# Attention on one core: where GpSimd splits the queries, and where it adds up the modulation

## The chip, the cores and the metric

One Trainium2 chip, one core. The metric is the time on the device in microseconds (us) of one execution. An execution takes 2790.1 us (median of 3, 2789.61 to 2793.39).

## What is computed

An encoder trunk of two layers on a sequence of 1024 positions, width 1024, in float32. The first layer mixes positions by grouped-query attention, the second by a gated unit; each is followed by a squared-ReLU MLP, and each sub-layer is normalised and modulated (shift, scale, gate) by a conditioning vector. What matters here, cut from the reference:

```python
cond = jax.nn.silu(c)
for i in range(DEPTH):                                   # 2
    mod = cond @ ada_w[i] + ada_b[i]                     # 6 x 1024 values
    sh1, sc1, g1, sh2, sc2, g2 = jnp.split(mod, N_MOD, axis=-1)
    ...
def one_block(q_blk):                                    # 16 heads of 64, 4 key heads
    s = jnp.einsum('bqkgd,bskd->bkgqs', q_blk, k).astype(jnp.float32) * scale
    p = jax.nn.softmax(s, axis=-1).astype(v.dtype)
    return jnp.einsum('bkgqs,bskd->bqkgd', p, v)
```

## The kernel before

TensorE multiplies operands of a reduced kind of float32, so every operand is split in two parts, a rounded one ("hi") and the rest ("lo"), and products of the parts are added in PSUM. Splitting is work for ScalarE, VectorE and GpSimd.

The attention loop (line 920) runs over 64 units. Unit i is one head and 256 queries; four units in a row (i mod 4 = 0 to 3) share one key head and one group of 256 queries. The stages of a unit are spread over three iterations, and the order of all instructions is written out by hand, in a string of twenty steps that each iteration goes through (line 1588):

```python
ORDER = "s00 v20 t10 q10 h10 t11 e00 s01 h11 t12 h12 v21 t13 e01 h13 v22 v23 q00 f20 m00"
```

The letter is the stage; the first digit says whose it is (0: unit i, 1: unit i-1, 2: unit i-2). Most instructions are pinned to this order; the split of the queries is not pinned, but instructions on one engine run one behind the other.

- s (line 834): scores, four matmuls of 512 columns; VectorE takes their maximum (line 837).
- e (line 843): the exponential, on ScalarE. t (line 851): its transposes on TensorE, copied by ScalarE to the rounded part (line 854). h (line 860): the rest, on VectorE.
- v (line 870): product with the values; ScalarE copies the two halves (lines 880 and 882), and f (line 887) joins them on GpSimd.
- q with w = 0, near the end of an iteration: `q_stage` on GpSimd, for the next group of four units. Per half of the 256 queries it makes the rounded part (line 811) and the rest (line 812), so four instructions per call, into two tiles of the pool "t" (58 tiles of 128x512).
- q with w = 1, near the start of the iterations with i mod 4 = 2 and 3: `q_trans`, four pinned transposes on TensorE (line 820) of what `q_stage` made, and a copy by ScalarE (line 823). The result is used from the next i mod 4 = 0 on.
- m, the last step of an iteration: first, in the opening units, some deferred work (rotary positions of the last queries: lines 567 and 569 on VectorE, 570 and 583 on GpSimd); in units 53 to 62 preparation for the output product; then `slabs.step`.

`slabs.step` works off 32 steps of the modulation of the second layer, four groups of eight. Where its second argument is true it takes one step:

```python
self.ahead(3)                                            # loads, 512 KB each, SP's queue
...
if dt == 0:
    pin(G.tensor_scalar(self.acc[g], raw, condc[:, 0:1], None, ALU.mult))            # line 182
else:
    pin(G.tensor_scalar(raw, raw, condc[:, dt : dt + 1], None, ALU.mult))            # line 184
    pin(G.tensor_tensor(self.acc[g], self.acc[g], raw, ALU.add))                     # line 185
```

`ahead(3)` keeps up to three loaded tiles (the present step's and two more), of four buffers. Three iterations after the eighth step of a group, eight small matmuls close it (line 194).

The q step with w = 0 stands ahead of f and m in an iteration. So on GpSimd a unit's order is: split (if any), join, deferred work, modulation step (if any).

Of the kernel before, what the change touches and what calls it, by code (L numbers as in the profile page):

```python
# [36 lines left out]
def encoder_kernel(ctx: ExitStack, tc: tile.TileContext, t: dict, out: bass.AP):  # L37
# [16 lines left out]
    def slot(dt=F32, shape=(P, 512)):  # L54
        return mem.tile(list(shape), dt, tag="t", name=nm("t"), bufs=SLOTS["t"])
# [24 lines left out]
    def f32(ap):  # L80
        return ap.bitcast(F32)
# [119 lines left out]
    slabs = Slabs([(1, 1), (1, 0), (1, 2), (1, 4)])  # L201

    def mods(n, tag="w"):
        for _ in range(min(n, len(pending))):
            layer, j, k = pending.pop(0)
            mod_load(layer, j, k, tag)
            if j in (1, 4):
                mod_scale(layer, j // 3, k)
# [252 lines left out]
    def load_x(hf, k):  # L461
        x_ = xslot()
        nc.sync.dma_start(x_, t["xT"][k * P : (k + 1) * P, hf * HALF : (hf + 1) * HALF])
        return x_
# [292 lines left out]
    def load_sel():  # L757
        for i in range(2):
            raw, s_ = slot(F32, (32, 512)), slot(F32R, (32, 512))
            nc.sync.dma_start(raw, t["sel"][:, i * 512 : (i + 1) * 512])  # L760
            V.tensor_copy(s_, raw)
            sel.append(s_)

    def wo_sums(hf):
        ri = small.tile([P, 4, NH], F32, tag="ri", name=nm("ri"), bufs=1)
        V.reciprocal(ri, rowsum[:, 4 * hf : 4 * hf + 4])
        rs = small.tile([P, 4, 2, NH], F32R, tag="rs", name=nm("rs"), bufs=1)
        V.tensor_copy(rs[:, :, 0], ri)
        V.tensor_tensor(rs[:, :, 1], ri, f32(rs[:, :, 0]), ALU.subtract)
        pt = bank_x("rt", (32, 512), F32R)  # L770
        for j in range(4):
            T.transpose(pt[:, j * P : (j + 1) * P], rs[:, j].rearrange("p s h -> p (s h)"), identr)
        rT[hf] = slot(F32R, (32, 512))
        S.copy(rT[hf], f32(pt))

    def wo_prep(hf, dt):
        pb = bank_x("bc")
        T.matmul(pb, sel[dt // 4][:, (dt % 4) * P : (dt % 4 + 1) * P], rT[hf], start=True, stop=True)
        o_ = ot.pop((dt, hf))
        V.tensor_tensor(o_, o_, pb, ALU.mult)  # L780
        hi, lo = slot(F32R), slot(F32R)
        S.copy(hi, o_)
        (G, V)[hf].tensor_tensor(lo, o_, f32(hi), ALU.subtract)
        on[(dt, hf)] = (hi, lo)

    def wo_mm(m, halves, bank):
        wh, wl = load_w("wo", m)
        ps = {hf: bank("wo") for hf in halves}
        for hf in halves:
            for k in range(KT):  # L790
                hi, lo = on[(k, hf)]
                T.matmul(ps[hf], wh[:, k], hi, start=k == 0, stop=False)
                T.matmul(ps[hf], wh[:, k], lo, start=False, stop=False)
                T.matmul(ps[hf], wl[:, k], hi, start=False, stop=k == KT - 1)
        for hf in halves:
            V.scalar_tensor_tensor(x[hf][m], ps[hf], mod[:, 0, 2, m : m + 1], x[hf][m], ALU.mult, ALU.add)
            (sqA, sqB)[hf].add(x[hf][m])
# [4 lines left out]
    with ExitStack() as es:  # L802

        def q_stage(qq, g):
            qh = []
            for j in range(2):
                q_ = qn[(2 * qq + j, g // 2)]
                src = q_[:, (g % 2) * 256 : (g % 2) * 256 + 256].rearrange("p (h d) -> p h d", h=4)
                d_ = slot(F32R)
                dv = d_.rearrange("p (h s d) -> p h s d", h=4, s=2)  # L810
                G.tensor_copy(dv[:, :, 0], src)
                G.tensor_tensor(dv[:, :, 1], src, f32(dv[:, :, 0]), ALU.subtract)
                qh.append(d_)
            return qh

        def q_trans(qh, hp, qst, bank=bank_x):
            pt = bank("qt", dt=F32R)
            for h in range(2):
                for j in range(2):
                    pin(T.transpose(pt[:, (2 * h + j) * P : (2 * h + j + 1) * P],  # L820
                                    qh[j][:, (2 * hp + h) * P : (2 * hp + h + 1) * P], identr))
            d_ = slot(F32R)
            pin(S.copy(d_, f32(pt)))
            qst.append(d_)
# [65 lines left out]
        units = []  # L890
# [7 lines left out]
        nu = len(units)  # L898

        qh = q_stage(0, 0)  # L900
# [19 lines left out]
        for i in range(nu + 2):  # L920
            u0 = units[i] if i < nu else None
            u1 = units[i - 1] if 0 < i <= nu else None
            u2 = units[i - 2] if i > 1 else None
            if u0:
                if i % 4 == 0:
                    qst, nxt = nxt, []
                u0.qst = qst
            for op in ORDER.split():
                f, w, j = op[0], int(op[1]), int(op[2])
                if f == "m":  # L930
                    if deferred:
                        deferred.pop(0)()
                    elif WO_AT <= i < WO_AT + 10:
                        if i == WO_AT:
                            load_sel()
                        elif i == WO_AT + 1:
                            wo_sums(0)
                        else:
                            wo_prep(0, i - WO_AT - 2)
                    elif i >= nu:  # L940
                        mods(1)
                    slabs.step(bank_x, i * 5 % 8 < 5)
                elif f == "q":
                    if i % 4 == 1 and w == 0 and i + 3 < nu:
                        qh = q_stage(units[i + 3].qq, units[i + 3].g)
                    if i % 4 > 1 and w == 1 and i + 2 < nu:
                        q_trans(qh, i % 4 - 2, nxt)
                else:
                    u = (u0, u1, u2)[w]
                    if u and (i or f not in "se"):  # L950
                        stages[f](u, j)
            if i == nu - 1:
                x[0] = [load_x(0, k) for k in range(KT)]
            if i == nu:
                wo_mm(0, (0,), bank_x)
# [308 lines left out]
    for ct in range(24):  # L1264
        i, r = divmod(ct, 3)
# [392 lines left out]
```

## Time and profile before

| | |
|---|---|
| median of 3 runs | 2790.1 us |
| profiled execution, its time | 2792.5 us |
| its span | 2790.5 us |
| mean granted clock of TensorE | 0.979 |
| TensorE busy, of the span | 2661.6 us, 95% |
| VectorE busy | 2269.1 us, 81% |
| ScalarE busy | 1459.8 us, 52% |
| GpSimd (POOL) busy | 1061.5 us, 38% |

"Busy" is the time in which an engine had an instruction in work. The granted clock is the share of TensorE's full clock that the chip allowed; at 0.5 a matmul takes twice as long. In the views of waits a row names who waited, at which line, and which engine and line ended the wait. In the timeline a row is one instruction or several alike (xN), with the idle time ahead of it in square brackets. PEld is TensorE's loading of the stationary operand, which runs beside the matmuls. The attention loop begins near 194 us and its last scores are made near 623 us.

### The profile page before, as it was taken

The numbers are of one execution on the slowest core, as the hardware profiler recorded it, in microseconds if no ns is written. First come the engines' busy times: TensorE is split into PE (matmuls) and PEld (weight loads), VectorE is DVE, ScalarE is ACT, GpSimd is POOL, SyncE is SP. The second block draws the span as 40 slices with busy tenths as digits, with TensorE's granted clock in tenths as the row PEclk, the third lists the DMA queues.
The fourth block names the chain that finished last, engine by engine and source line by source line (L and its number), as shares of the span: only waits on it lengthen the run. The fifth ranks groups of instructions, "written<-read, shape, count | busy, mean of one in ns | idle before, by whom it ended". The sixth has DMA issues, their size and how long they took to land. (4 is left out here: it accounts for less than half of the span.)

```text
span 2790.5 us, 37339 instructions
## 1 busy us (share of the span) xinstructions
PE 2661.6 (95%) x12804; PEld 2195.3 (79%) x12804; DVE 2269.1 (81%) x3191; ACT 1459.8 (52%) x2598; POOL 1061.5 (38%) x716
## 2 busy tenths in 40 slices
PE   7888999999899999999999999999999999999999
PEld 5667888888678887877778888887878688878877
DVE  7887777788888778998797777777998887788994
ACT  4447877893555555444453354444436554454442
POOL 2447656633520005452343355555551400034530
PEclk9899999999999999999999999999999999999999
DMA  7241111125245457744433245558732264478452
GB/s 260 68 144 39 50 50 54 33 91 178 79 157 193 146 187 288 276 171 149 147 121 108 95 157 178 178 182 298 285 117 87 85 206 162 145 255 290 151 194 75
DMA packets 200544, 427.52 MB, mean 153 GB/s; under 512 B 23137, under 2 KB 35425, under 8 KB 200354
## 3 DMA queue, kind: packets, MB, share of 16 engines
q1 hardware_dynamic: 173474, 387.37, 40.6%
q10 hardware_dynamic: 26880, 37.76, 3.7%
q8 instruction: 101, 1.65, 0.3%
q14 instruction: 89, 0.73, 0.1%
HBM read 306.56 MB, written 118.49 MB: 152 GB/s over the span
## 5 line engine op out<-in xcount | busy, mean ns | idle before, releaser
L1074 PE MATMUL out<-t,s 128*128 128x512 f32 x1232 | 486.8, 396 | 14.5 <-DVE t L288 14.5
L1073 PE MATMUL out<-t,s 128*128 128x512 f32 x1232 | 487.8, 396 | 8.8 <-ACT t L287 8.8
L1075 PE MATMUL out<-t,s 128*128 128x512 f32 x1232 | 485.9, 395 | 6.1 <-DVE s L1058 5.9
L415 PE MATMUL w<-t,s 128*128 128x512 f32 x1168 | 460.2, 395 | 0.5 <-ACT t L287 0.5
L416 PE MATMUL w<-t,s 128*128 128x512 f32 x1168 | 455.5, 391 | 1.4 <-DVE t L288 1.3
L417 PE MATMUL w<-t,s 128*128 128x512 f32 x1168 | 455.1, 390 | 1.0 <-DVE s L401 0.9
L288 DVE TENSOR_TENSOR t<-t,t 128x512 fp32r<-128x512 f32 x408 | 376.8, 937 | 29.4 <-ACT t L287 21.9
L287 ACT CAST t<-t 128x512 fp32r<-128x512 f32 x408 | 244.6, 618 | 154.5 <-DMA t<-hf 63.3
L400 ACT CAST s<-w 128x512 fp32r<-128x512 f32 x292 | 174.3, 619 | 227.4 <-PE w L417 155.5
L1074 PEld LDWEIGHTS out<-t,s 128*128 128x128 f32 x1232 | 234.8, 191 | 70.9 <-DVE t L288 21.8
L1073 PEld LDWEIGHTS out<-t,s 128*128 128x128 f32 x1232 | 234.7, 191 | 62.9 <-ACT t L287 13.9
L1075 PEld LDWEIGHTS out<-t,s 128*128 128x128 f32 x1232 | 234.7, 191 | 59.8 <-DVE s L1058 11.1
L401 DVE TENSOR_TENSOR s<-w,s 128x512 fp32r<-128x512 f32 x292 | 228.5, 791 | 62.9 <-ACT s L400 59.1
L1044 POOL TENSOR_TENSOR w<-w,t 128x512 f32<-128x512 f32 x32 | 51.6, 1615 | 558.9 <-DMA t<-hf 490.4
L416 PEld LDWEIGHTS w<-t,s 128*128 128x128 f32 x1168 | 219.4, 188 | 51.1 <-DVE t L288 6.5
L415 PEld LDWEIGHTS w<-t,s 128*128 128x128 f32 x1168 | 219.3, 188 | 50.1 <-issue 3.3
L1058 DVE TENSOR_TENSOR s<-t,s 128x512 fp32r<-128x512 f32 x240 | 216.0, 901 | 51.8 <-ACT s L1057 51.5
L417 PEld LDWEIGHTS w<-t,s 128*128 128x128 f32 x1168 | 219.2, 188 | 46.9 <-DVE s L401 2.1
L1057 ACT CAST s<-t 128x512 fp32r<-128x512 f32 x240 | 147.9, 621 | 190.9 <-PE out L1075 115.4
L837 DVE TENSOR_REDUCE mx<-s 128x1 f32<-128x1024 f32 x128 | 156.7, 1224 | 70.7 <-PE s L834 69.6
L860 DVE TENSOR_TENSOR t<-t,t 128x512 fp32r<-128x512 f32 x256 | 164.9, 684 | 22.2 <-ACT t L854 21.8
L854 ACT CAST t<-t 128x512 fp32r<-128x512 f32 x256 | 145.3, 592 | 39.5 <-PE t L851 37.1
(247 smaller groups left out, 5473.7 us busy)
## 6 DMA issues: line engine op xcount, KB each, us to landing
t<-hf SPq DMA_DIRECT2D x320, 256.0 KB, 4.5
hf<-c SPq DMA_DIRECT2D x156, 256.0 KB, 2.1
w<-in_wi_dram SPq DMA_DIRECT2D x64, 512.0 KB, 4.1
hf<-c ACTq DMA_DIRECT2D x96, 256.0 KB, 2.0
c<-in_ada_dram SPq DMA_DIRECT2D x36, 512.0 KB, 4.6
w<-in_adan_dram SPq DMA_DIRECT2D x32, 512.0 KB, 3.3
t<-in_wm_dram SPq DMA_DIRECT2D x64, 256.0 KB, 5.2
wf<-w SPq DMA_DIRECT2D x64, 256.0 KB, 3.2
```

The lines of the kernel that those rows point to most:

```text
L287: S.copy(hi, src)
L288: (eng or V).tensor_tensor(lo, src, f32(hi), ALU.subtract)
L400: S.copy(hi, src)
L401: V.tensor_tensor(lo, src, f32(hi), ALU.subtract)
L415: T.matmul(ps, hi[:, a], th, start=kt == 0, stop=False)
L416: T.matmul(ps, hi[:, a], tl, start=False, stop=False)
L417: T.matmul(ps, lo[:, a], th, start=False, stop=kt == 3)
L860: pin(V.tensor_tensor(lo, pt, f32(hi), ALU.subtract))
L1058: V.tensor_tensor(lo, src, f32(hi), ALU.subtract)
L1073: T.matmul(ps, hi[:, a], th, start=begin and kt == 0, stop=False)
L1074: T.matmul(ps, hi[:, a], tl, start=False, stop=False)
L1075: T.matmul(ps, lo[:, a], th, start=False, stop=end and kt == 3)
```

## The change

```diff
                     elif i >= nu:
                         mods(1)
-                    slabs.step(bank_x, i * 5 % 8 < 5)
+                    slabs.step(bank_x, i % 4 in (1, 2) or i % 8 == 3)
                 elif f == "q":
-                    if i % 4 == 1 and w == 0 and i + 3 < nu:
-                        qh = q_stage(units[i + 3].qq, units[i + 3].g)
+                    if i % 4 == 0 and w == 0 and i + 4 < nu:
+                        qh = q_stage(units[i + 4].qq, units[i + 4].g)
                     if i % 4 > 1 and w == 1 and i + 2 < nu:
                         q_trans(qh, i % 4 - 2, nxt)
```

`q_stage` for the next group of four is called in the first unit of a group instead of the second; 15 calls in both. The modulation steps were taken in the units with i mod 8 = 0, 2, 4, 5 and 7; they are now taken in those with i mod 8 = 1, 2, 3, 5 and 6. Both are five in eight units, until the 32 steps are done. `q_trans` stays where it was.

## Prediction, made before the changed kernel was run

> **What bounds the kernel now.** I read the page first, then the waits, then the attention stage unit by unit in the timeline, and last the busy table of single units. Rows of the page: engine, busy us, share, instructions.
>
> ```profile
> span 2790.5 us, 37339 instructions
> PE 2661.6 (95%) x12804; PEld 2195.3 (79%) x12804; DVE 2269.1 (81%) x3191; ACT 1459.8 (52%) x2598; POOL 1061.5 (38%) x716
> ```
>
> TensorE bounds the kernel as a whole, and GpSimd is busy for 38% only. An average over stages says nothing of a wait inside one stage, so the view of waits comes next (waiter, released by: us in total, times, longest).
>
> ```profile
> PEld qt L820 <- POOL t L812: 35.1, 25, 5.7
> PE qt L820 <- POOL t L812: 30.2, 24, 5.4
> ```
>
> L820 are the transposes of the split queries, pinned in TensorE's order; L812 is the last step of the split on GpSimd. So TensorE, the bound, stands still for 30.2 us because GpSimd, a mostly idle engine, is late. The timeline shows why. One stretch of GpSimd, then of TensorE, around unit 38 of the attention loop (time, busy us, engine, line):
>
> ```profile
> 450.85 0.72 POOL L887 TENSOR_TENSOR t<-t,t 64x256 f32<-64x256 f32 x1 [4.48 <-ACT t L882]
> 451.56 2.85 POOL L184 TENSOR_SCALAR w<-w,condc 128x1024 f32<-128x1024 f32 x1
> 454.49 2.39 POOL L185 TENSOR_TENSOR s<-s,w 128x1024 f32<-128x1024 f32 x1
> 456.83 0.74 POOL L811 CAST t<-t 128x256 fp32r<-128x256 f32 x2
> 457.54 1.40 POOL L812 TENSOR_TENSOR t<-t,t 128x256 fp32r<-128x256 f32 x2
> ```
>
> ```profile
> 458.31 0.28 PE L820 MATMUL qt<-identr,t 128*128 128x128 f32 x1 [1.74 <-POOL t L812]
> 459.00 0.45 PE L820 MATMUL qt<-identr,t 128*128 128x128 f32 x3 [0.40 <-POOL t L812]
> ...
> 459.92 2.06 PE L834 MATMUL s<-x,t 128*128 128x512 f32 x4
> ...
> 464.59 1.09 PE L834 MATMUL s<-x,t 128*128 128x512 f32 x4
> ```
>
> GpSimd first does the join of unit 36 (L887, 0.72 us), then a modulation step of unit 36 (L184 and L185, 451.56 to 456.88: 5.3 us), and only then the split of unit 37 (456.83 to 458.94: 2.1 us), whose transposes are due right at the start of unit 38. TensorE waits, and afterwards four score matmuls take 2.06 us where they take 1.09 us a little later. The busy table shows the same unit between a unit without and one with transposes (stretch, length, busy PE, PEld, DVE, ACT, POOL, then granted clock):
>
> ```profile
> 444.70:450.20 5.50, 5.50 (x42) 5.10 (x41) 4.93 (x7) 5.10 (x11) 1.59 (x2) 1.00 0.28 95
> 455.70:465.70 10.00, 7.86 (x46) 6.82 (x45) 5.03 (x6) 5.87 (x12) 9.22 (x8) 0.83 0.16 52
> 465.70:471.50 5.80, 5.80 (x46) 5.41 (x46) 4.94 (x6) 5.44 (x12) 0.73 (x1) 1.00 0.27 93
> ```
>
> A unit costs 5.5 us, with transposes 5.8, and there TensorE is busy throughout. The delayed one costs 10.0, and its clock was granted at 0.83 only.
>
> **The price of the delays.** I take the first score maximum of a unit (L837) as its start. Here are units 7, 35 to 40, 41 and 53:
>
> ```profile
> 247.49 1.23 DVE L837 TENSOR_REDUCE mx<-s 128x1 f32<-128x1024 f32 x1 [0.47 <-PE s L834]
> ...
> 438.87 1.23 DVE L837 TENSOR_REDUCE mx<-s 128x1 f32<-128x1024 f32 x1 [0.27 <-PE s L834]
> 444.69 1.23 DVE L837 TENSOR_REDUCE mx<-s 128x1 f32<-128x1024 f32 x1 [0.22 <-PE s L834]
> 450.19 1.23 DVE L837 TENSOR_REDUCE mx<-s 128x1 f32<-128x1024 f32 x1 [0.21 <-PE s L834]
> 455.70 1.23 DVE L837 TENSOR_REDUCE mx<-s 128x1 f32<-128x1024 f32 x1 [0.22 <-PE s L834]
> 465.72 1.23 DVE L837 TENSOR_REDUCE mx<-s 128x1 f32<-128x1024 f32 x1 [0.58 <-PE s L834]
> 471.54 1.22 DVE L837 TENSOR_REDUCE mx<-s 128x1 f32<-128x1024 f32 x1 [0.22 <-PE s L834]
> 478.83 1.23 DVE L837 TENSOR_REDUCE mx<-s 128x1 f32<-128x1024 f32 x1 [0.87 <-PE s L834]
> 555.03 1.23 DVE L837 TENSOR_REDUCE mx<-s 128x1 f32<-128x1024 f32 x1 [0.21 <-PE s L834]
> ```
>
> Units 36 and 37 take 5.50 and 5.51 us. Units 35 and 39 (i mod 4 is 3, second half of the transposes, never delayed) take 5.82. Unit 40, which closes a group of modulation sums with eight small matmuls, takes 7.29, that is 1.78 more than 5.51. Unit 38 takes 10.02, which is 4.20 too much: 2.1 us are waits (1.74 and 0.40), the other 2.1 us are slow matmuls behind them. From unit 7 to 53 there are 46 units, 23 of them with transposes, and three close a group. Without delays they would take 23 x 5.82 + 23 x 5.505 + 3 x 1.78 = 265.8 us. They took 555.03 - 247.49 = 307.5. So **41.7 us** of this stretch are delay, in the eleven units with i mod 4 = 2 from 10 to 50. This is more than the waits alone, because the slowed clock is in it.
>
> **The change part by part.** The split moves from the end of units 1, 5, 9... to the end of units 0, 4, 8...: the same 15 calls of four GpSimd instructions each, no DMA, nothing added. The modulation steps move from units 0, 2, 4, 5, 7 (mod 8) to 1, 2, 3, 5, 6: still five in eight, 32 in all, each with two GpSimd instructions (the first of a group one) and a 512 KB load on SP's queue.
>
> What GpSimd must do, by the durations above: step 5.3, join 0.73, split 2.1. In eight units that is 5 x 5.3 + 8 x 0.73 + 2 x 2.1 = 36.5 us, against 4 x 5.5 + 4 x 5.82 = 45.3 us that eight undelayed units take. It fits; the order decides.
>
> The split of i mod 8 = 4 is the tight one, as three steps in a row come before it. Count from the start of the unit after i mod 8 = 1. The join is released at +0.66 (450.19 to 450.85), so join and step end at 6.7; the second pair at 12.7; the third at 18.7 (6.03 each, longer than a unit, so a backlog builds). The split then ends at 20.8. The units passed are 5.82 + 5.82 + 5.5 + 5.5 = 22.6 us, and the transposes are due some 0.6 us into the next one, at about 23.2. It is ready **2.4 us early**. The split of i mod 8 = 0 has two steps and then an empty unit ahead of it: it ends at 15.5 on the same count, 7.7 us early. So all eleven delays go: -41.7 us. What is late next is nothing on GpSimd. Units then cost 5.82, as units 35 and 39 show, with TensorE busy throughout.
>
> The twelfth delay, the first in the stage, is different. At its start GpSimd also turns the last queries (L570, L583), and there the line-up is:
>
> ```profile
> 228.12 2.22 POOL L583 TENSOR_TENSOR t<-t,r 128x512 f32<-128x512 f32 x1
> ...
> 233.38 2.85 POOL L184 TENSOR_SCALAR w<-w,condc 128x1024 f32<-128x1024 f32 x1
> ...
> 238.59 0.75 POOL L811 CAST t<-t 128x256 fp32r<-128x256 f32 x2
> ...
> 240.08 0.37 PE L820 MATMUL qt<-identr,t 128*128 128x128 f32 x1 [5.41 <-POOL t L812]
> ```
>
> TensorE was ready at 234.7. Behind L583 (ends 230.34) the new order has the step of unit 3 (5.3, to 235.7), then the split. The first transpose started 1.5 us after the split's start (238.59 to 240.08), so it starts at 237.2: a wait of 2.5 us where there were 5.4. I take **-3 us**, with bounds 0 (the clock slows as before) and -6.8 (the whole delay of units 5 and 6 goes).
>
> The other edits cost nothing. The loads land in time:
>
> ```profile
> DMA to landing us min/median/max: 3.1/3.3/4.7
> ```
>
> Three steps in a row use one tile each 6.0 us, and each is requested two steps ahead; if that cover were gone a step would wait 3.3 us, beyond the 2.4 us in hand. The joins run up to 6 us later, but only the output product much later reads them. The four closings move by at most one unit and cost 1.78 us each as before.
>
> The slowed clock is where a rule can be weighed. The row of unit 38 shows 0.83 behind an idle time of 1.74 us. The Trainium skill (TensorE: Matmul & The Clock Gate, Part 1) says that the clock falls back after at least one idle window of about 3.4 us. By that rule gaps of 1.7 us would leave the clock alone, and the change would be worth the waits only; the row disagrees and I go by it.
>
> **Sum.** -41.7 - 3 = -44.7 us. The profiled execution took 2792.5 us (span 2790.5), so it would become 2747.8; against the median of 2790.1 that is **2745.4 us**. For the rest of the kernel I allow 4 us either way, as instructions that aren't pinned may shift; the forecast's own range is 2739 to 2753.
>
> **Rivals.**
> First, only the waits go and the slow clock stays, because it belongs to this stage and not to the waits. For: the matmuls of unit 38 stay slow well past the wait, beyond 459.92, so the slowness isn't the wait itself. Against: clock 1.00 in the undisturbed units above. It would give 30.2 less the 2.8 us still waited at the first split: 27.4, so 2762.7 us. The Trainium skill's window rule just cited points this way. Chance 0.08.
>
> Second, the three steps in a row eat the 2.4 us: the splits of i mod 8 = 4 stay late while those of 0 come free. That needs each step to take 0.8 us longer. Against:
>
> ```profile
> L583 POOL TENSOR_TENSOR t<-t,r x20: 1040/1047/2218, 81.6 to 232.4; 128x512 f32<-128x512 f32 x20
> L184 POOL TENSOR_SCALAR w<-w,condc x28: 2839/2846/2854, 220.5 to 545.1; 128x1024 f32<-128x1024 f32 x28
> ```
>
> The shortest and longest L184 (ns, minimum, median, maximum) are 0.5% apart wherever it ran. For: L583 took up to twice its median, once in the opening units (the 2.22 us above), so GpSimd work can slow. If late as now, five delays like unit 38's stay (at most 5 x 4.2 = 21 us): 2766 us. Chance 0.10. The Trainium skill (SBUF — State Buffer, Who interferes with whom) has GpSimd blocked by VectorE instructions with two SBUF inputs; L860 and L837, which read PSUM, wouldn't do it, so by that page this stage is safe.
>
> Third, on the slow side: the pool of 58 "t" tiles runs out. Each split holds two of them for one unit more; if none is free, the copy of the transposed weights (L854) waits a unit, 5.5 us, at each of 15 splits: +83, so 2790.1 - 44.7 + 83 = 2828 us. It decides from 3.0 us per split upwards (44.7 / 15). Against it is what L854 waits for now:
>
> ```profile
>   PE t L851: 37.1, 77
>   POOL s L185: 0.6, 2
> ```
>
> That is its own input, and hardly a freed tile. Chance 0.04.
>
> Fourth, the splits, which aren't pinned, are put behind the steps again, and nothing changes: 2790 us. Against: in all rows above they stand in the order of the program. Chance 0.03.
>
> **How the numbers follow.** Forecast 0.75, rivals 0.08, 0.10, 0.04, 0.03. The range takes the forecast's own range and reaches up to the first rival: 2738 to 2763, which leaves out the second rival, the last two and a little of the forecast. A measurement of this kernel tells about 0.2% (5.6 us) from no change. Forecast and first two rivals are faster by more: 0.93. Same 0.03, slower 0.04.
>
> **What would show it.** Right: the waits of qt L820 on POOL L812 fall from 30.2 to under 4 us, one near 235 us the longest; first score maxima of units 7 to 53 lie some 266 us apart; units of i mod 4 = 2 take 5.8 us at clock 1.00; GpSimd's busy time stays near 1061 us. Wrong: waits of 1 us or more at units 14, 22, 30, 38, 46 (second rival); clock below 1 between the waits (first); L854 waiting for a tile (third); L811 starting right behind L185 at units of i mod 4 = 2 (fourth).

## The result, and the profile after

The changed kernel takes **2743.78 us** (median of 4, 2740.23 to 2745.62), against 2789.86 before: ratio 0.9831, 95% interval 0.9814 to 0.9848. The forecast was 2745.4. The profiled execution took 2744.76 us, the page's first rows are:

```profile
span 2742.9 us, 37309 instructions
PE 2642.3 (96%) x12804; PEld 2184.9 (80%) x12804; DVE 2275.4 (83%) x3191; ACT 1454.5 (53%) x2598; POOL 1063.8 (39%) x716
```

GpSimd does the same work in the same time (1063.8 us against 1061.5); only its order is new. The view of the transposes' line (L820), its part on what they waited for:

```profile
its engine sat idle before it (us, times) until:
who waited for it (us, times):
```

Nothing stands under "sat idle": the 30.2 us of waits on the split are gone entirely. The starts of units 7, 38, 39 and 53 by their first score maximum, as shown for the kernel before:

```profile
243.81 1.23 DVE L837 TENSOR_REDUCE mx<-s 128x1 f32<-128x1024 f32 x1 [0.22 <-PE s L834]
...
422.79 1.23 DVE L837 TENSOR_REDUCE mx<-s 128x1 f32<-128x1024 f32 x1 [0.22 <-PE s L834]
428.61 1.23 DVE L837 TENSOR_REDUCE mx<-s 128x1 f32<-128x1024 f32 x1 [0.22 <-PE s L834]
...
509.68 1.23 DVE L837 TENSOR_REDUCE mx<-s 128x1 f32<-128x1024 f32 x1 [0.21 <-PE s L834]
```

Unit 38 now takes 428.61 - 422.79 = 5.82 us (10.02 before), what undelayed units with transposes took before. From unit 7 to 53 it is 265.87 us. The busy table of that stretch (length, PE, PEld, DVE, ACT, POOL, granted clock) has TensorE busy throughout and at full clock:

```profile
243.80:509.70 265.90, 265.90 (x1982) 247.70 (x1982) 229.45 (x284) 243.06 (x484) 200.02 (x149) 1.00 0.17 55
```

GpSimd around the tight split, that of unit 44 (44 mod 8 = 4), with the end of the third step ahead of it:

```profile
463.94 2.39 POOL L185 TENSOR_TENSOR s<-s,w 128x1024 f32<-128x1024 f32 x1
466.26 0.74 POOL L811 CAST t<-t 128x256 fp32r<-128x256 f32 x2
466.97 1.44 POOL L812 TENSOR_TENSOR t<-t,t 128x256 fp32r<-128x256 f32 x2
...
470.51 0.54 PE L820 MATMUL qt<-identr,t 128*128 128x128 f32 x4
```

The split ends at 468.41; its transposes start at 470.51 in unit 46, 2.1 us later. Where the time went, span against span: up to unit 7 the kernel is 247.49 - 243.81 = 3.7 us ahead, from unit 7 to 53 41.7 us, and in all that follows 2.3 us, which is within the spread of single runs. Together 47.6 us, of 2790.5 - 2742.9.

One thing is worse. In the opening, unit 3 takes 8.15 us (218.33 to 226.48). VectorE and GpSimd there:

```profile
218.33 1.21 DVE L837 TENSOR_REDUCE mx<-s 128x1 f32<-128x1024 f32 x1
...
223.59 2.97 DVE L569 TENSOR_TENSOR t<-t,t 128x256 f32<-128x256 f32 x2
223.88 2.39 POOL L185 TENSOR_TENSOR s<-s,w 128x1024 f32<-128x1024 f32 x1
...
226.48 1.21 DVE L837 TENSOR_REDUCE mx<-s 128x1 f32<-128x1024 f32 x1
```

The same place in the kernel before, where unit 3 took 5.93 us:

```profile
222.75 0.76 DVE L569 TENSOR_TENSOR t<-t,t 128x256 f32<-128x256 f32 x2
223.42 1.22 DVE L837 TENSOR_REDUCE mx<-s 128x1 f32<-128x1024 f32 x1
223.45 2.39 POOL L185 TENSOR_TENSOR s<-s,w 128x1024 f32<-128x1024 f32 x1
```

The two multiplies of L569 took 2.97 us instead of 0.76. Before, both were all but through (222.75 + 0.76 = 223.51) when L185 started on GpSimd at 223.45; after, L185 started between them, and the second ended only when L185 did. The score maximum queued behind it on VectorE came late, and ScalarE and TensorE behind it. The experiments had to settle two things: which half of the change does the work, and whether this reading of unit 3 holds.

### The profile page after: what moved, and what is told of

It is laid out like the page before. It is cut to its first block, busy times and chain, and to the rows that moved or that the text cites. A ratio compares the mean times of both kernels' runs of the same rounds, so it can differ in the third digit from the quotient of the medians.

```text
span 2742.9 us, 37309 instructions
## 1 busy us (share of the span) xinstructions
PE 2642.3 (96%) x12804; PEld 2184.9 (80%) x12804; DVE 2275.4 (83%) x3191; ACT 1454.5 (53%) x2598; POOL 1063.8 (39%) x716
## 5 line engine op out<-in xcount | busy, mean ns | idle before, releaser
L287 ACT CAST t<-t 128x512 fp32r<-128x512 f32 x408 | 244.3, 617 | 157.9 <-DMA t<-hf 65.2
L860 DVE TENSOR_TENSOR t<-t,t 128x512 fp32r<-128x512 f32 x256 | 164.3, 683 | 20.9 <-ACT t L854 20.9
L837 DVE TENSOR_REDUCE mx<-s 128x1 f32<-128x1024 f32 x128 | 156.6, 1224 | 23.7 <-PE s L834 22.4
L870 PE MATMUL o<-t,t 128*128 128x256 f32 x1024 | 163.7, 293 | 0.0
```

The costliest lines, as they stand in the source:

```text
L287: S.copy(hi, src)
L860: pin(V.tensor_tensor(lo, pt, f32(hi), ALU.subtract))
```

## The experiments

Medians below are of 4 or 5 runs. The kernel before had 2790.46 us in the first four runs and 2789.86 in the last four.

**Only the split moved.**

```diff
-                    slabs.step(bank_x, i % 4 in (1, 2) or i % 8 == 3)
+                    slabs.step(bank_x, i * 5 % 8 < 5)
```

(against the changed kernel, as are all diffs here)

> The split in units 0, 4, 8... as in the changed kernel, the modulation steps in units 0, 2, 4, 5, 7 (mod 8) as before. Theory A (a step that runs right ahead of the split on GpSimd is the whole cause, so either half of the change is enough): the tightest split (i mod 8 = 0) stands behind the step of unit 7, ends 8.8 us into unit 0 and is due at 11.6, so no wait: units 7 to 53 in 266 us. The opening has no step of unit 3 ahead of the rotary work, so it costs nothing there: 2741 us, some 3 us below the changed kernel. Theory B (both halves are needed, each gives about half): 2767 us, with waits of the transposes on the split left at about six units.

Measured: 2740.93 us, ratio 0.9825 (0.9812 to 0.9838). Units 7 and 53 of it:

```profile
243.26 1.23 DVE L837 TENSOR_REDUCE mx<-s 128x1 f32<-128x1024 f32 x1 [0.22 <-PE s L834]
...
509.45 1.22 DVE L837 TENSOR_REDUCE mx<-s 128x1 f32<-128x1024 f32 x1 [0.21 <-PE s L834]
```

266.2 us, no wait of the transposes on the split. Theory A holds, theory B falls. The opening didn't go as expected: unit 3 took 8.14 us here too, with the steps where they were before. So moving the steps isn't needed to slow it. That the median is still the 2741 us of theory A is luck: units 0 to 7 take 49.4 us here and in the changed kernel, and the 2.9 us between the two medians have no place in the loop.

The rows of units 2 and 3 show how the loss of unit 3 came about, first in the kernel before, then here:

```profile
216.82 0.76 DVE L569 TENSOR_TENSOR t<-t,t 128x256 f32<-128x256 f32 x2
216.95 1.22 POOL L887 TENSOR_TENSOR t<-t,t 64x256 f32<-64x256 f32 x1 [2.74 <-ACT t L882]
```

```profile
216.74 1.29 DVE L569 TENSOR_TENSOR t<-t,t 128x256 f32<-128x256 f32 x2
216.86 0.89 POOL L887 TENSOR_TENSOR t<-t,t 64x256 f32<-64x256 f32 x1 [2.73 <-ACT t L882]
...
223.21 2.96 DVE L569 TENSOR_TENSOR t<-t,t 128x256 f32<-128x256 f32 x2
223.50 2.39 POOL L185 TENSOR_TENSOR s<-s,w 128x1024 f32<-128x1024 f32 x1
```

Already in unit 2 the multiplies took 1.29 us instead of 0.76, beside the join (L887), which was the shorter this time (0.89 instead of 1.22 us). So VectorE came to the multiplies of unit 3 half a microsecond later (223.21 against 222.75), while L185 began when it had before (223.50 against 223.45), and now met them. Why the pair of unit 2 fell the other way isn't shown: the join began 0.13 us after the multiplies before, and 0.12 us here.

**Only the steps moved.**

```diff
-                    if i % 4 == 0 and w == 0 and i + 4 < nu:
-                        qh = q_stage(units[i + 4].qq, units[i + 4].g)
+                    if i % 4 == 1 and w == 0 and i + 3 < nu:
+                        qh = q_stage(units[i + 3].qq, units[i + 3].g)
```

> The modulation steps in units 1, 2, 3, 5, 6 (mod 8) as in the changed kernel, the split in units 1, 5, 9... as before. Theory A: the split of i mod 8 = 5 comes behind the third step of the row and one join more, ends at 21.5 us where 23.2 is due, so no wait in the steady part: units 7 to 53 in 266 us. Only the first one, behind the rotary work, waits about 1 us: 2745 us. Theory B: 2767 us.

Measured: 2746.49 us, ratio 0.9838 (0.9824 to 0.9851). The first split and units 7 and 53:

```profile
239.60 0.28 PE L820 MATMUL qt<-identr,t 128*128 128x128 f32 x1 [0.65 <-POOL t L812]
240.28 0.45 PE L820 MATMUL qt<-identr,t 128*128 128x128 f32 x3 [0.40 <-POOL t L812]
...
245.38 1.22 DVE L837 TENSOR_REDUCE mx<-s 128x1 f32<-128x1024 f32 x1 [0.20 <-PE s L834]
...
511.25 1.23 DVE L837 TENSOR_REDUCE mx<-s 128x1 f32<-128x1024 f32 x1 [0.21 <-PE s L834]
```

The steady part takes 265.9 us again, and the first split waits 1.05 us, as expected. Unit 3 took 8.12 us here too, with the split where it was before. So the two halves do not add: each alone removes all eleven delays of the steady part, and the second adds nothing to the first there.

**Two steps in unit 3, none in unit 6.**

```diff
-                    slabs.step(bank_x, i % 4 in (1, 2) or i % 8 == 3)
+                    slabs.step(bank_x, (0, 1, 1, 2, 0, 1, 0, 0)[i % 8])
...
-            if not go or not self.work:
-                return
-            self.ahead(3)
+            for _ in range(min(go, len(self.work))):
+                self.one()
+
+        def one(self):
+            self.ahead(3)
```

> The changed kernel, but unit 3 (mod 8) takes two modulation steps and unit 6 none; the same 32 steps, the same five in eight units. By the time in hand that the prediction worked out (2.4 us for the split of i mod 8 = 4), this split now ends 5.3 us later, 2.9 us after it is due, in about six groups. Theory A with a clock that slows behind a wait: six times 2.9 us of wait and about 2 us of slow matmuls, 29 us: 2773 us, the clock below 1.00 only in units with i mod 8 = 6. If only the wait counts: 2761 us. If the time in hand was wrong and GpSimd has more of it: 2744 us.

Measured: 2766.55 us (2761.32 to 2769.1), ratio 0.9907 (0.9893 to 0.992): 22.8 us above the changed kernel's median, between the two sizes expected. TensorE's transposes at unit 22 in the timeline (their line is L822 here), then the busy table of that unit:

```profile
340.49 0.37 PE L822 MATMUL qt<-identr,t 128*128 128x128 f32 x1 [2.27 <-POOL t L814]
341.17 0.62 PE L822 MATMUL qt<-identr,t 128*128 128x128 f32 x3 [0.32 <-POOL t L814]
```

```profile
337.30:349.00 11.70, 9.11 (x47) 8.04 (x46) 5.03 (x6) 6.06 (x12) 10.43 (x9) 0.71 0.14 48
```

A step put ahead of the split brings the delays back, by about the lateness worked out: waits of 2.6, 2.6 and 2.7 us at units 22, 38 and 46, where 2.9 were forecast. Unit 22 lost 11.70 - 5.82 = 5.9 us, so 3.3 us of it are matmuls at the slow clock; unit 46 lost 4.7. From unit 7 to 53 it is 17.9 us more than in the changed kernel (283.73 against 265.87), and 6.2 us are lost ahead of unit 7, where unit 6 waits 4.2 us. The total is smaller than 29 us, since two of the six groups of units (those of units 14 and 30, which lost 0.7 and 0.8 us) hold a shorter step, the first of its group, which is one instruction instead of two; I had not counted that.

**No step before unit 5.**

```diff
-                    slabs.step(bank_x, i % 4 in (1, 2) or i % 8 == 3)
+                    slabs.step(bank_x, i > 4 and (i % 4 in (1, 2) or i % 8 == 3))
```

> The changed kernel, with no modulation step before unit 5, so the 32 steps end in unit 54 instead of 50. In the changed kernel unit 3 takes 8.15 us, where it took 5.93 before; one VectorE multiply of the rotary work (L569) lasts 2.63 us there instead of 0.42, having started 0.04 us behind the second instruction of a modulation step (L185). Theory C (VectorE is held off by that instruction): without steps in units 0 to 4 unit 3 takes 5.9 us and unit 7 starts near 240.5 instead of 243.8: 2740.5 us. Rival D (units 2 to 4 are slow for another reason, such as the queue of the rotary work on GpSimd): unit 3 stays near 8 us, 2744 us.

Measured: 2743.71 us (2740.07 to 2744.59), ratio 0.9828 (0.9815 to 0.9842). The multiply of unit 3 and the start of unit 7:

```profile
222.65 1.29 DVE L569 TENSOR_TENSOR t<-t,t 128x256 f32<-128x256 f32 x2
...
240.59 1.23 DVE L837 TENSOR_REDUCE mx<-s 128x1 f32<-128x1024 f32 x1 [0.20 <-PE s L834]
```

Unit 7 starts at 240.59, where theory C had it, but 0.9 us of the 3.2 were there when the loop began (193.52 against 194.44); from unit 3 to 7 it takes 23.2 us, 25.5 in the changed kernel. Unit 3 takes 6.5 us and not 5.9, as the multiplies still take 1.29 us, now beside the joins (L887). So 1.7 of the 2.2 us that unit 3 had lost hang on the early steps, as theory C has it. The median, though, is the one that rival D gave: a gain of 2.3 us doesn't show in a total whose runs spread over 4.5 us.

**The changed kernel again**, as the yardstick for the following three.

> The changed kernel once more, as the yardstick for the three that share its runs: 2743.8 us, with a spread of 3 us either way in the part behind the attention loop, which no variant touches.

Measured: 2743.27 us (2741.03 to 2744.57), ratio 0.983 (0.9817 to 0.9843).

**The split one unit earlier still.**

```diff
+        qh = q_stage(units[4].qq, units[4].g)
         for i in range(nu + 2):
...
-                    if i % 4 == 0 and w == 0 and i + 4 < nu:
-                        qh = q_stage(units[i + 4].qq, units[i + 4].g)
+                    if i % 4 == 3 and w == 0 and i + 5 < nu:
+                        qh = q_stage(units[i + 5].qq, units[i + 5].g)
```

> The changed kernel with the split one unit earlier still (units 3, 7, 11..., and the first one ahead of the loop), so that two tiles of the pool of 58 are held for one unit more at each of 15 splits. Theory A (the split has time in hand already, and tiles are plenty): units 7 to 53 in 266 us, the same total as the changed kernel. Third rival of the prediction (the pool runs out, a unit of 5.5 us lost at each split): up to 83 us more, 2827 us, with waits of the copy of the transposed weights (L854).

Measured: 2744.04 us, ratio 0.9834 (0.982 to 0.9847), the yardstick's time. Units 7 to 53 take 265.9 us (244.32 to 510.19). All that L854 waited for:

```profile
  PE t L851: 27.4, 57
```

The copy waits for its own input and for nothing else; the pool has tiles to spare, and the third rival falls.

**Products first, additions from unit 5 on.**

```diff
-                pin(G.tensor_tensor(self.acc[g], self.acc[g], raw, ALU.add))
+                self.adds.append((g, raw))
+            while late and self.adds:
+                g_, raw_ = self.adds.pop(0)
+                pin(G.tensor_tensor(self.acc[g_], self.acc[g_], raw_, ALU.add))
...
-                    slabs.step(bank_x, i % 4 in (1, 2) or i % 8 == 3)
+                    slabs.step(bank_x, i % 4 in (1, 2) or i % 8 == 3, i > 4)
```

> The changed kernel, where the steps of units 1 to 3 do only their product (one input, L182 or L184); the additions (two inputs) follow in unit 5. Theory C, narrowed (VectorE's two-input multiply is held off only by a GpSimd instruction with two inputs): unit 3 takes 6.5 us as in the run without early steps, and unit 7 starts some 1.7 us earlier than in the changed kernel: 2742 us. Wider theory (any GpSimd instruction that reads SBUF holds it off): one of the multiplies of units 2 to 4 lasts 2 us or more beside a product, unit 3 stays near 8 us, 2744 us.

Measured: 2739.62 us (2738.13 to 2742.47), ratio 0.9819 (0.9806 to 0.9832), the fastest of all. Its opening (L570 is here the multiply called L567 above, L840 the score maximum, of units 3 and 7):

```profile
218.09 1.21 DVE L840 TENSOR_REDUCE mx<-s 128x1 f32<-128x1024 f32 x1
...
220.69 2.85 POOL L184 TENSOR_SCALAR w<-w,condc 128x1024 f32<-128x1024 f32 x1
...
222.75 0.68 DVE L570 TENSOR_TENSOR t<-t,t 128x512 f32<-128x512 f32 x1
...
240.96 1.22 DVE L840 TENSOR_REDUCE mx<-s 128x1 f32<-128x1024 f32 x1 [0.20 <-PE s L837]
```

From unit 3 to 7 it takes 22.9 us, against 25.5 in the yardstick (219.24 to 244.69): 2.6 us less. The product L184 ran all through L570, which took its usual 0.68 us. So this one-input product did not hold VectorE, and taking L185 away from the multiply takes most of the loss away (unit 3 takes 6.5 us). That no one-input instruction of GpSimd holds it is not shown: in this run the two casts of the split, beside the multiplies of unit 4, took 1.08 us together where they take 0.74 alone, and those multiplies 0.95 us where they take 0.75. The median is 3.7 us below the yardstick's, with ranges that overlap (its slowest 2742.47, the yardstick's fastest 2741.03); 2.6 us of it have a place in the trace.

**The split moved, the steps as before but from unit 5 on.**

```diff
-                    slabs.step(bank_x, i % 4 in (1, 2) or i % 8 == 3)
+                    slabs.step(bank_x, i > 4 and i * 5 % 8 < 5)
```

> The split in units 0, 4, 8..., the steps in the units of the kernel before (0, 2, 4, 5, 7 of eight) but from unit 5 on. Theories A and C: units 2 to 4 take 6.5 us each, unit 7 starts near 240.6, units 7 to 53 take 266 us: 3 us less than the changed kernel, 2740.5 us. If the gain of 3 us at unit 7 is given back later (the steps now reach into the units that prepare the output product): the same as the changed kernel.

Measured: 2748.32 us (2745.91 to 2749.91), ratio 0.9848 (0.9835 to 0.9862): 5 us above the yardstick. Neither case had that: the gain of the opening (units 0 to 7 take 2.2 us less than in the yardstick) is given back, and more. Unit 58, where the last group of sums is now closed beside the preparation of the output product (L109 is a split of its weights on GpSimd, L198 the closing on VectorE):

```profile
550.27 2.37 POOL L109 TENSOR_TENSOR s<-w,s 128x1024 fp32r<-128x1024 f32 x1 [4.80 <-PE am L194]
550.42 2.23 DVE L198 SCALAR_TENSOR_TENSOR amod<-mod,ng 128x8 f32<-128x8 f32 x1
552.58 1.21 DVE L837 TENSOR_REDUCE mx<-s 128x1 f32<-128x1024 f32 x1
```

An instruction on 8 columns took 2.23 us, where it took 0.60 at the other closing of this run that has it; L109 had started 0.15 us ahead of it. Unit 58 took 9.5 us (543.04 to 552.58; 6.4 in the changed kernel, which has its closing elsewhere). This looks like the loss of unit 3 over again with another pair, and the run without steps before unit 5 has it too: in its unit 57 L198 took 2.32 us, L109 having started 0.10 us ahead. From unit 53 to 63 this run takes 2.7 us more than the yardstick. Another 1.9 us lie between units 7 and 53, in units 32 and 33 behind a closing. There the clock was below 1.00 without any wait on the split, with TensorE busy throughout:

```profile
391.40:399.60 8.20, 8.20 (x49) 7.60 (x49) 6.22 (x8) 4.34 (x8) 6.51 (x4) 0.79 0.19 60
```

What slowed it there isn't shown, and the rest of the 5 us I did not place.

## Why the prediction was right, and where it wasn't

- **The eleven delays.** Forecast 41.7 us from unit 7 to 53, 265.8 us without them; measured 41.7 and 265.9. The sum over unit starts was right because it counts whatever a delay costs, wait or slow clock.
- **The time in hand of the tight split.** Forecast 2.4 us, measured 2.1 at unit 44; with one step more ahead of the split it turned into waits of 2.6 and 2.7 us where 2.9 were forecast. The second rival is answered by this: the steps took 2.85 and 2.39 us as before.
- **Both halves as one.** The prediction costed the change as a whole and did not see that either half would do; the first two experiments show it.
- **The first delay.** Forecast -3 us, measured -3.7 up to unit 7, but not by the steps given. I expected a remaining wait of 2.5 us at unit 6, and units 2 to 5 as before. The start of unit 6 before, then the split and unit 6 after:

```profile
234.00 1.23 DVE L837 TENSOR_REDUCE mx<-s 128x1 f32<-128x1024 f32 x1
```

```profile
234.83 0.75 POOL L811 CAST t<-t 128x256 fp32r<-128x256 f32 x2
...
237.99 1.23 DVE L837 TENSOR_REDUCE mx<-s 128x1 f32<-128x1024 f32 x1 [0.21 <-PE s L834]
...
238.62 0.54 PE L820 MATMUL qt<-identr,t 128*128 128x128 f32 x4
```

  The split began at 234.83, 0.9 us earlier than worked out (235.7), but TensorE came to unit 6 4.0 us later than before, 2.2 of it lost in unit 3, and waited for nothing. Unit 6 became 7.7 us shorter (13.49 to 5.82) and units 2 to 5 together 3.7 us longer; that the two come near -3 is luck. The failed step is the sentence that this stage is safe from VectorE and GpSimd holding each other off. I had weighed the steady instructions, L860 and L837, and overlooked the multiplies of the opening, whose two inputs both lie in SBUF. The Trainium skill (SBUF — State Buffer, Who interferes with whom) says just this of them: a VectorE instruction with two SBUF inputs contends with GpSimd's reads, and the one that starts first has its way. L569 after L185 and L198 after L109 agree with it; L567 beside L184 does not, as it kept its 0.68 us beside a product that reads one tensor from SBUF. The other way round was in the prediction's own rows: the L583 of 2.22 us, given there only as a sign that GpSimd can slow, began at 228.12, just behind the first of these two rows of the kernel before, and a usual one takes 1.05 us:

```profile
228.07 0.69 DVE L567 TENSOR_TENSOR t<-t,t 128x512 f32<-128x512 f32 x1
228.67 0.76 DVE L569 TENSOR_TENSOR t<-t,t 128x256 f32<-128x256 f32 x2
```

- **The slow clock (first rival).** After, 1.00 over the whole stretch: it went with the waits. But a wait doesn't always bring it. Unit 46 of the kernel before had the same waits as unit 38 (1.74 and 0.41 us), and its busy row is

```profile
507.80:516.20 8.40, 6.25 (x46) 5.48 (x46) 4.93 (x6) 5.70 (x12) 8.14 (x8) 1.00 0.20 63
```

  with the clock at 1.00 and 1.6 us less than unit 38's 10.0. So the price of such a wait of 2.1 us was 2.6 us in the one and 4.2 in the other, and only a sum over many is safe. By the window rule of the Trainium skill that the prediction weighed (TensorE: Matmul & The Clock Gate, Part 1) a wait of 1.7 us would have slowed neither. The row of unit 38 goes against that and the row of unit 46 doesn't. What slows the clock stays open: in the last run it fell to 0.79 with no wait on the split.
- **Slower or unchanged (third and fourth rival).** Tiles were plenty; the splits stand where the program puts them.

## What to carry to other kernels

When the bound engine waits for an engine that is 38% busy, look at what stands right ahead of the awaited work in that engine's queue: here, moving a long step out of the way or the awaited work one unit forward was worth the same, and the second of the two added nothing. Price such a delay by the distance of two marks that enclose it, not by its wait, as the slow clock behind it can double it (4.2 us for 2.1 at unit 38). And look at which instructions run side by side when work moves on GpSimd: a long two-input instruction there can hold a short one of VectorE with two inputs in SBUF until it ends.

## What the runs showed of the hardware

- VectorE's multiply of two SBUF operands (128x256) lasts 0.42 us alone and up to 2.63 us when GpSimd's two-input addition on 128x1024 has started just before; the two rows of L569, in ns, minimum, median and maximum, before and after:

```profile
L569 DVE TENSOR_TENSOR t<-t,t x32: 364/423/1507, 75.7 to 229.0; 128x256 f32<-128x256 f32 x32
L569 DVE TENSOR_TENSOR t<-t,t x32: 360/419/2633, 74.7 to 232.1; 128x256 f32<-128x256 f32 x32
```

- GpSimd's one-input product on as many columns (2.85 us) held no such multiply in the openings shown here.
- Tenths of a microsecond settled what the multiplies of unit 3 took: begun 0.70 us ahead of L185 (222.75 against 223.45, before) 0.76 us, begun 0.29 us ahead of it (223.21 against 223.50, with only the split moved) 2.96 us.
